# A planner's times set to the trace, and its projections handed out pass by pass

## Chip, cores and metric

One core of a Trainium2 chip runs the whole program. The metric is the time of one execution on the device in microseconds. The kernel before takes 1763.38 us, the median of three runs (1762.12 to 1763.65). The execution that was profiled took 1761.48 us, and its trace, from the first to the last instruction, spans 1759.5 us.

## The reference

Input x is 512 tokens by 1024 channels, fp32. Two transformer layers and a third block run one after the other:

```python
for i in range(2):                                   # first_block
    h, mem_n = _rms_norm(x, ...), _rms_norm(mem, ...)
    if i == 0:  # dilated band attention (12 heads) + attention on 256 memory tokens
        mixed = _attention_sublayer(h, mem_n, att_w_in, att_w_out, rel_bias, mem_w_kv[0])
    else:       # gated delta rule, 6 heads of 128, both directions, chunks of 64, + memory
        mixed = _deltanet_sublayer(h, mem_n, dn_w_in, dn_conv, ..., dn_w_out, mem_w_kv[1])
    x = x + _rms_norm(mixed, ...)
    h = _rms_norm(x, ...)
    x = x + _rms_norm(_swiglu(h, ffn_w_gate_up[i], ffn_w_down[i]), ...)   # width 2816
# second_block: one layer, three mixers beside each other
proj = rmsnorm(x, norm_g) @ w_in
y_gla = gla_mixer(...)      # gated linear attention, chunks of 32
y_s5 = s5_mixer(...)        # diagonal state space, scan over 512 tokens
y_nsa = nsa_mixer(...)      # compressed, selected and windowed attention
x = x + concat(y_gla, y_s5, y_nsa) @ w_out
```

In the delta rule each head solves a unit triangular system per chunk and then carries a state from chunk to chunk, in both directions:

```python
v_new = uc - wc @ state
out = (qc * exp(gc)) @ state + ac @ v_new
state = state * exp(g_last) + (kc * exp(g_last - gc)).T @ v_new
```

## The kernel before, in words

Every large product is done in three fp32r passes: each operand is split into a high and a low part, and `mm3` (L268 to L273) issues low weights by high activations, high by low, and high by high into one PSUM bank. A projection of a piece of 128 output columns over 512 tokens is eight such steps, one for each 128 rows of the weight. The weights come from HBM in pieces of 512 KB, and `weight_stream` (L217) has ScalarE make the high part (L243) and VectorE the low part (L262; GpSimd for a few pieces that are marked `aside`).

No instruction is placed by hand. `Flow` (L56) is a planner that runs while the program is built. Each piece of work is a generator, a thread, which says before each of its steps on which engine it runs and how long it takes (`yield "PE", 0.65`, or `yield act(512)`, `dve(512)`, `pool(512)`, L151 to L160), and issues the step's instructions when the planner hands it on. The planner holds a clock for each engine. A step can start when its engine is free and its inputs are there, which is the end of the producing step plus `HOP`, 0.2 us, where the producer is another engine (`start`, L93; 0.07 us on the same engine, none on TensorE). Of all steps on offer `run` (L99) takes the engine whose step can start first; of that engine's steps that can start within `DELTA`, 0.1 us, of it, the one with the lowest due number (`late`). What comes out is the order of the instructions in each engine's queue. The engines take their queues strictly in that order, and each waits on semaphores for its inputs: the planner's times set the order and nothing else. Rotating buffers and PSUM banks are counted by the same planner (`quota`, `get`, `put`).

The stages: layer 0's attention with its projections (to about 240 us of the trace), its output projection and feed-forward part (to 640), layer 1's delta rule (to 1000), its output projection and feed-forward part (to 1400), the second block (to the end). In the feed-forward stages TensorE has one thread of work. In the delta rule and in the second block, the mixed stages, the `projector` (L1788) is a thread with the due number 20 that offers its projections whenever nothing more urgent can start; the mixers' threads have due numbers from about -9 to 6. Its inner function `part` yields one step for the three passes of an `mm3`, 0.65 us for 512 columns. The output projection and the feed-forward part (`tok_proj`, L967, thread `trunk` with due number 50) yield 0.68 us for an `mm3` and are not touched.

In the delta rule, `inverse` (L1486 on) solves a head's triangular systems in 64 by 64 tiles (L1519 to L1548 by turns of TensorE, ScalarE and VectorE). `chain` carries the state, two threads a head, one for each direction. One chunk of it is

```python
matmul(b[:, 0:P], kT[:, cs], St)                   # PE   L1594
scalar_tensor_tensor(rh, b[:, 0:P], neg, vt, ...)  # DVE  L1597, declared 0.26
matmul(b[:, P:2 * P], Uf[:, d, c, :], rh)          # PE   L1602, declared MM = 0.22
activation(vn, b[:, P:2 * P], AF.Copy)             # ACT  L1605, declared act(128) = 0.21
tensor_scalar(vs, vn, col(ksc, d, c, h), ...)      # DVE  L1610, declared 0.14
matmul(b[:, 2 * P:3 * P], kt[:, c, :], vs)         # PE   L1612
```

and `query` multiplies AT and qe on GpSimd (L1454, L1456, declared `pool(512)` = 1.33). `norm_chain` (L906) ends each sublayer: for each of four groups of 128 tokens a few small VectorE operations (L917, L919, declared 0.1 and 0.07), one on GpSimd (L921, declared 0.47), 512-wide ones on VectorE and ScalarE, again a small one and one on GpSimd (L935, L938), and then TensorE transposes (L949).

Of the kernel before, what the change touches and what calls it, by code (L numbers as in the profile page):

```python
# [49 lines left out]
        self.h, self.l = hi, lo  # L50


DELTA = 0.1


class Flow:  # L56
# [3 lines left out]

    HOP = 0.2

    def __init__(self, **sets):
        self.free = dict.fromkeys(("PE", "ACT", "DVE", "POOL", "DMA"), 0.0)
# [26 lines left out]
    def start(self, eng, toks):  # L93
        s = self.free[eng]
        for at, e in toks:
            s = max(s, at + (self.HOP if e != eng else 0.0 if e == "PE" else 0.07))
        return s

    def run(self):  # L99
        while self.threads:  # L100
            again = True
            while again:
                again = False
                for t in list(self.threads):
                    kind, *arg = t["req"]
                    value = None
                    if kind == "get" and any(self.sets[n] for n in arg):
                        value = min((n for n in arg if self.sets[n]), key=lambda n: min(self.sets[n])[0])
                        tok = min(self.sets[value])
                        self.sets[value].remove(tok)  # L110
                    elif kind == "two" and len(self.sets[arg[0]]) > 1:
                        for _ in range(2):
                            tok = min(self.sets[arg[0]])
                            self.sets[arg[0]].remove(tok)
                    elif kind == "wait" and all(e["tok"] for e in arg):
                        tok = max((e["tok"] for e in arg), key=lambda x: x[0])
                    elif kind == "move" and self.sets[arg[0]]:
                        src, dst = arg
                        tok = min(self.sets[src])
                        self.sets[src].remove(tok)  # L120
                        self.put(dst, tok)
                        tok = t["tok"]
                    elif kind == "late":
                        t["late"] = arg[0]
                        tok = t["tok"]
                    else:
                        continue
                    if tok[0] > t["tok"][0]:
                        t["tok"] = tok
                    self.step(t, value or tok)  # L130
                    again = True
            ops = []
            for t in self.threads:
                if t["req"][0] in self.free:
                    eng, cost, *after = t["req"]
                    ops.append((self.start(eng, after or [t["tok"]]), t))
            assert ops or not self.threads, ([(t["gen"].__name__, t["req"]) for t in self.threads], self.sets, self.free)
            if not ops:
                return
            s, t = min(ops, key=lambda x: x[0])  # L140
            s, t = min((x for x in ops if x[1]["req"][0] == t["req"][0] and x[0] <= s + DELTA), key=lambda x: x[1]["late"])
            eng, cost = t["req"][:2]
            self.free[eng] = s + cost
            t["tok"] = (s + cost, eng)
            self.step(t, t["tok"])
# [17 lines left out]
class K:  # L163
# [132 lines left out]
    def inputs(self, F, W, eX, eM, eF, pro):  # L296
# [93 lines left out]
        def memory():  # L390
            yield "late", 0.5
            for l in range(2):
                yield "wait", *eN[l]
                for c in range(2):
                    ev = W["mk"][l][c]
                    yield "wait", ev
                    yield "get", "mm"
                    p = self.psum("mm")
                    w = ev["W"]
                    for k in range(KT):  # L400
                        t = yield "PE", 0.33
                        self.mm3(p[:, :256], (w.h[:, k, :], w.l[:, k, :]), (M[l].h[:, k, :], M[l].l[:, k, :]),
                                 k == 0, k == KT - 1)
                    F.put("wsl", t)
                    F.add(evac(self.memK[l][:, c, :], p), 0.5, t)
                yield "wait", *W["mv"][l]
                for u in range(2):
                    yield "get", "mm"
                    p = self.psum("mm")
                    ts = slice(u * P, (u + 1) * P)  # L410
                    for k in range(KT):
                        w, kk = W["mv"][l][k // 4]["W"], k % 4
                        t = yield "PE", 0.33
                        self.mm3(p[:, :256], (M[l].h[:, k, ts], M[l].l[:, k, ts]), (w.h[:, kk, :], w.l[:, kk, :]),
                                 k == 0, k == KT - 1)
                    F.add(evac(self.memV[l][:, u, :], p, l == 1 and u == 1), 0.5, t)
                for _ in range(2):
                    F.put("wsl", t)
# [120 lines left out]
    def attention(self, F, W, eX, eM, eB, at, e2):  # L539
# [41 lines left out]
        def group(g):  # L581
# [37 lines left out]
            for i, t0 in enumerate((0, 64, 192, 320, 384)):  # L619
                yield "get", "mm"  # L620
                p = self.psum("mm")
                for k in range(KT):
                    w, kk = W2[k // 4]["W"], k % 4
                    t = yield "PE", 0.33
                    self.mm3(p[:, :256], (X.h[:, k, t0:t0 + P], X.l[:, k, t0:t0 + P]), (w.h[:, kk, :], w.l[:, kk, :]),
                             k == 0, k == KT - 1)
                F.add(copy_v(g, i, p[:, :256], r["t"][2][:, i, :], "mm"), g - 0.5, t)
# [394 lines left out]
    def out_ffn(self, F, i, W, gnext, groups, kev, before):  # L1022
# [57 lines left out]
        for part, (f0, f1) in enumerate(self.PARTS):  # L1080
# [22 lines left out]
            while f < nf:  # L1103
                fs = (f, f + 1) if part == 0 and f == 0 else (f,)
                banks = {}
                for hv in ((0, 256), (256, 512)) if len(fs) == 2 else ((0, 512),):
                    t0, t1 = hv
                    for u in range(t0 // P, t1 // P):
                        yield "wait", eX[u]
                    for f_ in fs:  # L1110
                        for z in range(2):
                            ev = gu[part][f_][z]
                            yield "wait", ev
                            if (f_, z) not in banks:
                                nm = yield "get", *self.ANY
                                banks[f_, z] = self.psum("bk"), nm
                            p = banks[f_, z][0]
                            for k in range(KT):
                                tk = yield "PE", 0.65 * (t1 - t0) / 512
                                self.mm3(p[:, t0:t1], (ev["W"].h[:, k, :], ev["W"].l[:, k, :]),  # L1120
                                         (X.h[:, k, t0:t1], X.l[:, k, t0:t1]), k == 0, k == KT - 1)
                            if t1 == S:
                                F.put("wsl", tk)
                        if t1 == S:
                            F.add(evac_gu(f_, (banks[f_, 0], banks[f_, 1], tk)))
                f += len(fs)
                if part == 0 and f == 4:
                    yield "DMA", 1.4
                    r["post"], _ = row("rowA", a["norm_ffn_post"][i])
                    yield "DMA", 1.4  # L1130
                    r["gain"], _ = row("rowB", gnext)
                    r["ev"] = [F.event() for _ in range(4)]
                    r["eX"] = [F.event() for _ in range(4)]
                    r["store"] = True
                    n4[:] = [0] * 4
# [634 lines left out]
    def proj(self, F, ev, eX, m=P):  # L1770
# [7 lines left out]
        for t0, t1 in rngs:  # L1778
            yield "wait", *eX[t0 // P:t1 // P]
            for k in range(KT):  # L1780
                t = yield "PE", 0.65 * (t1 - t0) / S
                self.mm3(p[:m, t0:t1], (W.h[:, k, :], W.l[:, k, :]), (X.h[:, k, t0:t1], X.l[:, k, t0:t1]),
                         k == 0, k == KT - 1)
        F.put("wsl", t)
# [3 lines left out]
    def projector(self, F, items, eX, eP, late=20, haste=0):  # L1788
# [3 lines left out]

        X = self.X
        yield "late", late

        def part(it, t0, t1):
            W, m = it["W"], it["args"][4]
            yield "wait", *eX[t0 // P:t1 // P]  # L1800
            for k in range(KT):
                t = yield "PE", 0.65 * (t1 - t0) / S
                self.mm3(it["p"][:m, t0:t1], (W.h[:, k, :], W.l[:, k, :]), (X.h[:, k, t0:t1], X.l[:, k, t0:t1]),
                         k == 0, k == KT - 1)
            if t1 == S:
                F.put("wsl", t)
                it["done"]["tok"] = t
# [11 lines left out]
        for i, it in enumerate(items):  # L1819
# [13 lines left out]
            for u in range(4):  # L1833
# [3 lines left out]
                sl = slice(u * P, (u + 1) * P)  # L1837
                for k in range(KT):
                    W, kk = it[k // 4]["W"], k % 4
                    t = yield "PE", 0.33  # L1840
                    self.mm3(p[:, :256], (X.h[:, k, sl], X.l[:, k, sl]), (W.h[:, kk, :], W.l[:, kk, :]),
                             k == 0, k == KT - 1)
                evac, late_ = it[0]["use"]["f"]
# [392 lines left out]
    def s5(self, F, W, eX, open_, eY, uT):  # L2236
# [140 lines left out]
        def glu():  # L2377
# [14 lines left out]
            for c in range(2):  # L2392
                zs = []
                for o in (2, 0):
# [1 line left out]
                    p = self.psum("lv", "glu")  # L2396
                    os_ = slice((o + c) * P, (o + c + 1) * P)
                    for k in range(2):
                        t = yield "PE", 0.65
                        self.mm3(p, (w.h[:, k, os_], w.l[:, k, os_]), yh[k], k == 0, k == 1)  # L2400
                    zs.append((p, t))
                if c:
# [896 lines left out]
```

## Time and profile before

| | |
|---|---|
| median of three runs | 1763.38 us |
| the profiled execution | 1761.48 us |
| its span, first to last instruction | 1759.5 us |
| mean granted TensorE clock | 0.993 of 2.4 GHz |
| TensorE, matmuls | 1708.7 us busy (97%) |
| VectorE | 979.8 us (56%) |
| ScalarE | 763.2 us (43%) |
| GpSimd | 338.0 us (19%) |

Matmuls are pipelined and their ends are modelled: the record of one reaches past the start of the next, and the distance from start to start says what a pass takes of the engine. A short wait of TensorE hides in that overlap, and only a longer one shows as idle time. PE is TensorE's matmuls, PEld its weight loads, DVE VectorE, ACT ScalarE, POOL GpSimd. In names such as bk<-Xh,wl the output stands first, then what is streamed and what is loaded.

### The profile page before, as it was taken

The page shows a single profiled execution, that of the slowest core. Times are in us where ns is not written, and L with a number is a line of the kernel's source. Part 1 is how long each engine was busy: PE and PEld are TensorE (multiplying, and loading weights), DVE is VectorE, ACT ScalarE, POOL GpSimd, SP SyncE. Part 2 cuts the span into 40 slices and gives each one's busy share as a digit, 9 for nine tenths or more (in the row PEclk, how much of TensorE's full clock was granted, in tenths as well). Part 3 has the DMA queues.
Part 4 walks back from the last instruction along what each step waited for, and adds up shares of the span by engine and source line. Part 5 has one row for each costly group of instructions (what it writes and reads, how often), then busy time and mean ns, then how long its engine had stood idle before and what let it go on. Part 6 is the DMA issues. An engine that isn't in the chain of part 4 may idle for free.

```text
span 1759.5 us, 30190 instructions
## 1 busy us (share of the span) xinstructions
PE 1708.7 (97%) x12031; PEld 1423.2 (81%) x12031; DVE 979.8 (56%) x1997; ACT 763.2 (43%) x1808; POOL 338.0 (19%) x496
## 2 busy tenths in 40 slices
PE   6999999999999999999999899999999999999999
PEld 5988679888888888788777788888888888888787
DVE  6333656323333378867887467464433468467573
ACT  5443635333223245656555355333223353345671
POOL 5200001000000021220222351364540033210000
PEclk9999999999999999999999999999999999999999
DMA  6513133333233332211110164345333253552012
GB/s 195 154 51 95 49 120 97 120 96 96 96 96 96 96 114 79 61 38 38 38 37 32 59 152 139 109 133 144 108 108 96 77 159 115 153 154 69 25 37 84
DMA packets 211981, 167.84 MB, mean 95 GB/s; under 512 B 21996, under 2 KB 183036, under 8 KB 211840
## 3 DMA queue, kind: packets, MB, share of 16 engines
q1 hardware_dynamic: 203808, 154.39, 29.7%
q0 software_dynamic: 4560, 9.42, 2.1%
q10 hardware_dynamic: 3472, 2.10, 0.4%
q8 instruction: 94, 1.54, 0.4%
q14 instruction: 47, 0.39, 0.1%
HBM read 152.23 MB, written 13.65 MB: 94 GB/s over the span
## 4 chain that ended last, share of the span: by engine, by line
PE 84%; DVE 9%; ACT 2%; issue 2%; DMA 1%; POOL 1%; ACTq 0%; SPq 0%; DVEq 0%; POOLq 0%
PE bk L271 23%; PE bk L272 22%; PE bk L273 22%; DVE hn L1324 2%; DVE wl L262 1%; PE no L2753 1%; PE npT L2736 1%; PE x L1519 1%; PE x L1523 1%; PE y L1544 1%; DVE hs L942 1%; PE ns L2722 1%; PE hT L949 1%; PE ns L2720 1%; PE o L1625 1%
## 5 line engine op out<-in xcount | busy, mean ns | idle before, releaser
L262 DVE TENSOR_TENSOR wl<-raw,wh 128x512 fp32r<-128x512 f32 x450 | 315.8, 742 | 372.4 <-ACT wh L243 371.8
L243 ACT ACTIVATE wh<-raw 128x512 fp32r<-128x512 f32 x474 | 273.0, 623 | 534.4 <-PE bk L273 300.4
L271 PE MATMUL bk<-Xh,wl 128*128 128x512 f32 (+2 forms) x1312 | 494.9, 377 | 0.2 <-ACT Xh L951 0.2
L272 PE MATMUL bk<-Xl,wh 128*128 128x512 f32 (+2 forms) x1312 | 478.4, 365 | 0.5 <-DVE Xl L956 0.5
L273 PE MATMUL bk<-Xh,wh 128*128 128x512 f32 (+2 forms) x1312 | 478.5, 365 | 0.0
L273 PEld LDWEIGHTS bk<-Xh,wh 128*128 128x128 f32 (+1 forms) x1312 | 246.9, 188 | 40.1
L271 PEld LDWEIGHTS bk<-Xh,wl 128*128 128x128 f32 (+1 forms) x1312 | 247.5, 189 | 39.0 <-issue 3.5
L272 PEld LDWEIGHTS bk<-Xl,wh 128*128 128x128 f32 (+1 forms) x1312 | 247.7, 189 | 34.8 <-DVE Xl L956 0.9
L271 PE MATMUL bk<-wh,Xl 128*128 128x512 f32 (+1 forms) x424 | 152.6, 360 | 6.7 <-DVE Xl L796 3.7
L272 PE MATMUL bk<-wl,Xh 128*128 128x512 f32 (+1 forms) x424 | 145.8, 344 | 0.3 <-DVE wl L262 0.2
L273 PE MATMUL bk<-wh,Xh 128*128 128x512 f32 (+1 forms) x424 | 145.2, 342 | 0.0
L271 PE MATMUL bk<-wh,Al 128*128 128x512 f32 x352 | 139.7, 397 | 0.0
L272 PE MATMUL bk<-wl,Ah 128*128 128x512 f32 x352 | 139.5, 396 | 0.0
L921 POOL TENSOR_TENSOR nc<-ncm,nhalf 128x1 f32<-128x1 f32 x16 | 11.5, 720 | 661.9 <-DVE ncm L919 661.9
L273 PE MATMUL bk<-wh,Ah 128*128 128x512 f32 x352 | 138.6, 394 | 0.0
L1093 DVE TENSOR_TENSOR sg<-sg,bk 128x512 f32<-128x512 f32 x44 | 30.2, 687 | 124.7 <-PE bk L273 120.2
L271 PEld LDWEIGHTS bk<-wh,Xl 128*128 128x128 f32 x424 | 84.7, 200 | 18.0 <-DVE Xl L796 3.1
L273 PEld LDWEIGHTS bk<-wh,Xh 128*128 128x128 f32 x424 | 84.8, 200 | 8.1
L272 PEld LDWEIGHTS bk<-wl,Xh 128*128 128x128 f32 x424 | 85.0, 200 | 7.6 <-DVE wl L262 1.0
L271 PEld LDWEIGHTS bk<-wh,Al 128*128 128x128 f32 x352 | 66.0, 188 | 16.1
L273 PEld LDWEIGHTS bk<-wh,Ah 128*128 128x128 f32 x352 | 66.0, 188 | 16.0
L272 PEld LDWEIGHTS bk<-wl,Ah 128*128 128x128 f32 x352 | 66.1, 188 | 15.4
(586 smaller groups left out, 2623.8 us busy)
## 6 DMA issues: line engine op xcount, KB each, us to landing
raw<-in_ffn_w_gate_up_dram SPq DMA_DIRECT2D x88, 512.0 KB, 3.9
raw<-in_ffn_w_down_dram SPq DMA_DIRECT2D x44, 512.0 KB, 3.3
raw<-in_dn_w_in_dram SPq DMA_DIRECT2D x27, 512.0 KB, 4.0
raw<-in_att_w_in_dram SPq DMA_DIRECT2D x20, 512.0 KB, 4.1
raw<-in_w_in_dram SPq DMA_DIRECT2D x20, 512.0 KB, 3.8
raw<-in_mem_w_kv_dram SPq DMA_DIRECT2D x8, 512.0 KB, 3.6
raw<-in_att_w_out_dram SPq DMA_DIRECT2D x8, 512.0 KB, 3.3
xd<-x SPq DMA_DIRECT2D x8, 512.0 KB, 2.6
```

Of the source, the lines that this page charges most:

```text
L243: nc.scalar.activation(wh[:, sl], ev["raw"][:, sl], AF.Copy)
L262: eng.tensor_tensor(wl[:, sl], raw[:, sl], wh[:, sl].bitcast(F32), op=OP.subtract)
L271: mm(out, A[1], B[0], start=first, stop=False, **kw)
L272: mm(out, A[0], B[1], start=False, stop=False, **kw)
L273: mm(out, A[0], B[0], start=False, stop=last, **kw)
L942: nc.vector.scalar_tensor_tensor(hh[:, hv[i]], x[:, t, hv[i]], r2, r["gain"][:, hv[i]], op0=OP.mult, op1=OP.mult)
L949: nc.tensor.transpose(p[:, k * P:(k + 1) * P], hh[:, i * 512 + k * P:i * 512 + (k + 1) * P], self.ident)
L1093: nc.vector.tensor_tensor(sg, sg, pu, op=OP.mult)
L1324: nc.vector.scalar_tensor_tensor(acc[:, d0:d1], raw[:, d0 + o:d1 + o], cw[:, ti, tap:tap + 1], acc[:, d0:d1], op0=OP.mult, op1=OP.add)
L1519: nc.tensor.matmul(dn8(b[i])[at], lhsT, rhs, start=True, stop=True)
L1523: nc.tensor.transpose(b[d][:, o:o + P], U[:, d, 2 * n:2 * n + 2, :].rearrange("p c q -> p (c q)"), self.ident)
L1544: nc.tensor.matmul(dn8(ys[par])[HB[f], d, n, :], T[d][HB[par], n, f, :], xs[f][HB[par], d, n, :], start=True, stop=True)
```

## The change

The planner's numbers are replaced: `DELTA` 0.05 for 0.1; between engines 0.2 us from TensorE, 0.12 us to TensorE and 0.04 us otherwise, and nothing on the same engine; each step on VectorE costs 0.08 us and each on ScalarE 0.07 us more than it says; an `mm3` of 512 columns is 0.682 us (was 0.65), of 256 columns in the token-major projections 0.36 us (was 0.33). GpSimd's and the DMAs' declared times and the numbers that steps of the mixers declare for TensorE stay. In `projector`, `part` yields for each pass by itself, so that the planner can put other TensorE steps between the passes of one product; the passes, their order among themselves and their banks are the same.

```diff
-DELTA = 0.1
+DELTA = 0.05
...
-    HOP = 0.2
+    HOP = 0.04
+    FROM_PE, TO_PE = 0.2, 0.12
+    STEP = {"DVE": 0.08, "ACT": 0.07}
...
     def start(self, eng, toks):
         s = self.free[eng]
         for at, e in toks:
-            s = max(s, at + (self.HOP if e != eng else 0.0 if e == "PE" else 0.07))
+            s = max(s, at + (self.FROM_PE if e == "PE" else self.TO_PE if eng == "PE" else self.HOP) * (e != eng))
...
             eng, cost = t["req"][:2]
+            cost += self.STEP.get(eng, 0.0)
             self.free[eng] = s + cost
...
# front, token-major projections, projector's token-major pieces
-                        t = yield "PE", 0.33
+                        t = yield "PE", 0.36
...
# gate/up projections, proj, glu
-                t = yield "PE", 0.65 * (t1 - t0) / S
+                t = yield "PE", 0.682 * (t1 - t0) / S
...
# projector
         def part(it, t0, t1):
             W, m = it["W"], it["args"][4]
             yield "wait", *eX[t0 // P:t1 // P]
             for k in range(KT):
-                t = yield "PE", 0.65 * (t1 - t0) / S
-                self.mm3(it["p"][:m, t0:t1], (W.h[:, k, :], W.l[:, k, :]), (X.h[:, k, t0:t1], X.l[:, k, t0:t1]),
-                         k == 0, k == KT - 1)
+                for i, (w, x) in enumerate(((W.l, X.h), (W.h, X.l), (W.h, X.h))):
+                    t = yield "PE", 0.2275 * (t1 - t0) / S
+                    nc.tensor.matmul(it["p"][:m, t0:t1], w[:, k, :], x[:, k, t0:t1], start=k == i == 0,
+                                     stop=k == KT - 1 and i == 2)
```

## Rows read from the trace of the kernel before

**Rows 1.** The page's head, and its busy times by engine.

```profile
span 1759.5 us, 30190 instructions
PE 1708.7 (97%) x12031; PEld 1423.2 (81%) x12031; DVE 979.8 (56%) x1997; ACT 763.2 (43%) x1808; POOL 338.0 (19%) x496
```

**Rows 2.** By stage: stretch, length, then busy us by engine, clock, DMA, GB/s.

```profile
200.00:240.00 40.00, 33.02 (x281) 24.64 (x280) 30.00 (x75) 21.52 (x72) 0.00 (x0) 0.96 0.09 28
240.00:640.00 400.00, 399.56 (x1858) 331.70 (x1857) 158.43 (x262) 132.55 (x257) 7.79 (x12) 1.00 0.34 104
640.00:690.00 50.00, 44.23 (x296) 39.56 (x295) 41.63 (x82) 26.38 (x63) 12.63 (x12) 0.97 0.43 121
690.00:1000.00 310.00, 299.50 (x3656) 245.98 (x3654) 235.39 (x538) 174.67 (x477) 68.92 (x56) 0.99 0.14 40
1440.00:1715.00 275.00, 273.06 (x2476) 227.28 (x2475) 182.01 (x405) 148.78 (x392) 38.64 (x43) 1.00 0.35 98
```

**Rows 3.** Groups by line, 690 to 1000: count, busy us and mean ns, idle before.

```profile
L271 PE MATMUL bk<-Xh,wl 128*128 128x512 f32 x170 | 76.2, 448 | 0.0
L1612 PE MATMUL chain<-vs,ktok 128*128 128x128 f32 x72 | 14.5, 297 | 5.4 <-DVE vs L1610 5.3
```

**Rows 4.** TensorE in order of time: start, duration, line, instruction.

```profile
800.67 0.40 PE L273 MATMUL bk<-Xh,wh 128*128 128x512 f32 x1
800.90 0.38 PE L1594 MATMUL chain<-St,kTh 128*128 128x128 f32 x2
...
801.84 0.50 PE L271 MATMUL bk<-Xh,wl 128*128 128x512 f32 x1
802.18 0.39 PE L272 MATMUL bk<-Xl,wh 128*128 128x512 f32 x1
```

**Rows 5.** Waits of TensorE, 690 to 1000: us in total, times, longest.

```profile
PE chain L1612 <- DVE vs L1610: 5.3, 5, 1.4
```

**Rows 6.** Line L1610 in the whole trace: shortest, median and longest duration.

```profile
L1610 DVE TENSOR_SCALAR vs<-vn,ksc x36: 269/280/1299, 744.6 to 993.6; 128x128 f32<-128x128 f32 x36
```

**Rows 7.** A stall in order of time: TensorE, then VectorE, then GpSimd.

```profile
942.13 0.49 PE L1612 MATMUL chain<-vs,ktok 128*128 128x128 f32 x2 [1.33 <-DVE vs L1610]
...
940.79 2.50 DVE L1610 TENSOR_SCALAR vs<-vn,ksc 128x128 f32<-128x128 f32 x2
...
940.28 1.71 POOL L1456 TENSOR_TENSOR qe<-qe,qTh 128x512 f32<-128x512 f32 x1
941.95 1.26 POOL L1454 TENSOR_TENSOR AT<-AT,kq 128x512 f32<-128x512 f32 x1
```

**Rows 8.** A stretch of low clock, columns of rows 2, and TensorE in it.

```profile
864.50:867.80 3.30, 3.30 (x28) 2.79 (x30) 2.43 (x7) 0.79 (x2) 0.00 (x0) 0.50 0.00 0
943.10:946.40 3.30, 3.05 (x13) 2.84 (x14) 3.27 (x7) 0.28 (x1) 1.33 (x2) 0.50 0.00 0
...
865.08 0.63 PE L272 MATMUL bk<-Xl,wh 128*128 128x512 f32 x1
865.50 0.63 PE L273 MATMUL bk<-Xh,wh 128*128 128x512 f32 x1
```

**Rows 9.** One turn of the state's chain, in order of time.

```profile
987.47 0.39 PE L1594 MATMUL chain<-St,kTh 128*128 128x128 f32 x2
...
987.73 0.28 ACT L1605 ACTIVATE vn<-chain 128x128 f32<-128x128 f32 x1 [0.70 <-PE chain L1602]
...
988.16 0.28 DVE L1610 TENSOR_SCALAR vs<-vn,ksc 128x128 f32<-128x128 f32 x1
```

**Rows 10.** A norm chain in order of time, and its GpSimd step's group.

```profile
644.20 0.15 DVE L919 TENSOR_SCALAR ncm<-ncm 128x1 f32<-128x1 f32 x1
644.50 0.54 POOL L921 TENSOR_TENSOR nc<-ncm,nhalf 128x1 f32<-128x1 f32 x1 [0.94 <-DVE ncm L919]
645.08 1.77 DVE L925 SCALAR_TENSOR_TENSOR x<-y,nc,x 128x512 f32<-128x512 f32 x1
...
L921 POOL TENSOR_TENSOR nc<-ncm,nhalf 128x1 f32<-128x1 f32 x16 | 11.5, 720 | 661.9 <-DVE ncm L919 661.9
```

More of the change, by code (lines that the diff above doesn't have):

```diff
@@ L412, in memory @@
                         w, kk = W["mv"][l][k // 4]["W"], k % 4
-                        t = yield "PE", 0.33
+                        t = yield "PE", 0.36
                         self.mm3(p[:, :256], (M[l].h[:, k, ts], M[l].l[:, k, ts]), (w.h[:, kk, :], w.l[:, kk, :]),
@@ L623, in group @@
                     w, kk = W2[k // 4]["W"], k % 4
-                    t = yield "PE", 0.33
+                    t = yield "PE", 0.36
                     self.mm3(p[:, :256], (X.h[:, k, t0:t0 + P], X.l[:, k, t0:t0 + P]), (w.h[:, kk, :], w.l[:, kk, :]),
@@ L1118, in out_ffn @@
                             for k in range(KT):
-                                tk = yield "PE", 0.65 * (t1 - t0) / 512
+                                tk = yield "PE", 0.682 * (t1 - t0) / 512
                                 self.mm3(p[:, t0:t1], (ev["W"].h[:, k, :], ev["W"].l[:, k, :]),
@@ L1788, in projector @@
     def projector(self, F, items, eX, eP, late=20, haste=0):
-        X = self.X
+        X, nc = self.X, self.nc
         yield "late", late
@@ L1839, in projector @@
                     W, kk = it[k // 4]["W"], k % 4
-                    t = yield "PE", 0.33
+                    t = yield "PE", 0.36
                     self.mm3(p[:, :256], (X.h[:, k, sl], X.l[:, k, sl]), (W.h[:, kk, :], W.l[:, kk, :]),
@@ L2398, in glu @@
                     for k in range(2):
-                        t = yield "PE", 0.65
+                        t = yield "PE", 0.682
                         self.mm3(p, (w.h[:, k, os_], w.l[:, k, os_]), yh[k], k == 0, k == 1)
```

## The prediction

> **What bounds the kernel now.** I read the page's head first, then busy time by stage, then inside the mixed stages the waits of TensorE and the order of time around the longest. The head shows TensorE with matmuls in flight for 1708.7 of 1759.5 us [rows 1], so 50.8 us of idle is all that shows. By stage it is uneven: the feed-forward stretch has 0.4 us of it in 400, the delta rule 10.5 in 310 (690 to 1000), the norms at 640 to 690 5.8, the attention's end at 200 to 240 7.0, the second block's mixed part 1.9 in 275 [rows 2]. VectorE, the next engine, is at 235.4 of 310 in the delta rule [rows 2]. So the kernel is bound by TensorE's queue nearly everywhere, and a new order can win only what TensorE loses by standing before an instruction whose input is late while other work lies behind it. The start, the attention's end and the tail run out of such work: no order of projections helps there.
>
> Idle shows only part of the loss. A pass of 512 columns is recorded with 0.40 us, yet the next instruction starts 0.23 later [rows 4]; a wait under about 0.17 us hides in that overlap.
>
> What makes TensorE stand in the delta rule? Half of the 10.5 us is five waits at L1612 for VectorE's L1610, 5.3 us [rows 5]. L1610 takes 0.28 us in the median and 1.30 at worst [rows 6]. In the instance at 942 two of them stretch over 2.50 us while GpSimd runs L1456 and L1454, and TensorE idles 1.33 us before L1612 [rows 7]. After such waits TensorE's clock is at the half level, 1.2 GHz, at 864.5 and 943.1 [rows 8]. In the first, passes follow at 0.42 us instead of 0.23 [rows 4, 8], so 3.3 us of dense work lose 3.3 x (1 - 0.23/0.42) = 1.5.
>
> **The change, part by part.** No instruction is added or taken away: each `mm3` already was three matmuls with three weight loads, and the passes stay in order. Splitting costs nothing by itself where a 128-row small matmul follows a pass: L1594 starts 0.23 us behind L273, as another pass would [rows 4]. Behind the 64 by 64 tiles the first pass takes 0.34 us (801.84 to 802.18 [rows 4]), 0.11 more; each burst of these tiles is one step of the planner's and stays one, so that their number does not grow. I take 0. Bounds: 0, and 0.11 for each of the 170 `mm3` of [rows 3] if a border cost that wherever one is cut, 19 us; the nearer row, an ordinary small matmul, says 0.
>
> The split shortens how long an urgent step stands behind a projection: on average half a step, 0.34 us before and 0.11 after. That is latency of the mixers' chains, which TensorE's filler covers as long as projections last, so I cost it at nothing. Without that cover it would be 0.23 us a visit.
>
> `DELTA`: the planner may leave TensorE idle for up to 0.1 us so that an urgent step goes first, now 0.05. The mean of what can be left is 0.05 and 0.025. L1612's 72 records are 36 turns [rows 3, 9], and a turn has about four TensorE visits, so some 140 visits in the chains. If half of them used the allowance: 70 x 0.025 = 1.7 us won. Bounds 0 and 140 x 0.05 = 7.
>
> The times between engines: a round trip TensorE, VectorE, TensorE is planned with 0.2 + 0.08 + 0.12 = 0.40 us around the operation, 0.2 + 0.2 before: the same. With ScalarE and VectorE between (vn, vs) from the product to the end of vs: 0.2 + 0.28 + 0.04 + 0.22 = 0.74, before 0.2 + 0.21 + 0.2 + 0.14 = 0.75; the trace has 988.16 + 0.28 - 987.47 = 0.97 [rows 9]. So the new table is no nearer there. What it does mend is the load of VectorE and ScalarE, 0.08 and 0.07 us on every step that stood back to back, and projections 5% longer. From this I expect that part of the 5.2 us of delta-rule idle that isn't L1612's goes: I take two fifths, 2.0 us. Bounds: 5.2 won, and as much lost if new mis-orders replace the old.
>
> The collisions of L1610 with GpSimd: the planner keeps each engine's time by itself, before and after, so a new order shifts them by chance. I take 0 for the 5.3 us, bounds 5.3 won and 5.3 lost, with one half-clock stretch more or less for each pair of long waits: 2 x 1.5 either way. The page of the Trainium skill titled SBUF — State Buffer (SBUF: two separate sides) says that VectorE and GpSimd share one pair of ports as an exclusive lock, held for a whole instruction. The stretch of L1610 to 2.50 us for two beside L1456 agrees. By that rule no table of per-engine times can plan these waits away; by the planner's own table they would be gone, and the sum would be 5.3 + 3.0 us lower.
>
> The half-clock stretches: if fewer waits leave one of the two out, 1.5 us; I give it a half, 0.7. The second block has the same edits and 1.9 us of idle: I take 0.5 won, bounds 1.9 won and 3 lost.
>
> The norm chains: VectorE to GpSimd to VectorE was planned as 0.27 + 0.67 = 0.94 us from L919's start to L925's, now 0.19 + 0.51 = 0.70; the trace has 0.88 (644.20 to 645.08) [rows 10]. The transposes behind it may thus be queued 0.18 us too early, twice a chain, 16 chains [rows 10]: 5.8 us lost at most. Against it stands VectorE's longer planned load in the same stretch (41.6 of 50 us busy [rows 2]), which puts them later again. I take 0. If that cover is absent, transposes wait in front of gate/up passes.
>
> The remaining edits, 0.36 and 0.682 in the front and the gate/up stage, act where TensorE has one thread or is dense (399.6 of 400 [rows 2]): 0, bounds 2 either way.
>
> Sum: 1.7 + 2.0 + 0.7 + 0.5 = 4.9 us off the profiled execution, 1761.5 - 4.9 = 1756.6. That execution lies 1.9 below the median of the runs, so 1758.5 for the median.
>
> **Rivals.** *Nothing measurable*: chains that advance faster gain nothing where projections fill in, and the waits that cost are collisions that the table doesn't hold. For it: TensorE's 1.9 us of idle in 275 of the second block [rows 2], and L1612's half of the delta rule's idle [rows 5]. Against it: every queue of the mixed stages is reordered, so exact balance would be chance. 1763, within 3.5.
>
> *A tighter plan stalls more*, the slower side. An urgent step used to stand behind a whole `mm3` in the plan, and that margin, anything from 0 to 0.68 us, absorbed what came late. With passes it is 0 to 0.23. For an input late by 0.2 us (0.97 measured against 0.74 planned [rows 9]) the mean uncovered wait was 0.2 x 0.2/2/0.68 = 0.03 us and becomes 0.09. Over 140 visits 8 us, and with one half-clock stretch more about 9.5: 1772.9. It decides where lateness passes about 0.1 us, half a pass. For it: L1610's waits show that lateness of this size is there. Against it: many waits of 0.1 us hide or vanish in other lateness, and 0.05 less `DELTA` works the other way.
>
> *The collisions fall apart too*: the order moves the chains off GpSimd's L1454 and L1456, and L1612's waits and both half-clock stretches go: 1758.5 less 5.3 and the remaining 2.3 = 1750.9. For it: only five waits make the 5.3 us, so a small shift can miss them. Against it: GpSimd is busy 68.9 of 310 us [rows 2], and VectorE is loaded three quarters, so most shifts meet it again.
>
> *The change doesn't do what it says*: if no urgent step falls between the passes of one `mm3`, only the numbers act; this gives the time of the first rival and is counted with it.
>
> **How the numbers follow.** My forecast 0.34, collisions gone 0.12, nothing 0.25, tighter plan 0.29. About 0.2%, 3.5 us, is what a measurement of this kernel tells from no change. The forecast lies 4.9 below the median, just past that, so some of it falls inside; some of the first rival falls outside on either side. Faster 0.45, same 0.26, slower 0.29. Range: from 1745, below the collision rival by the bound of `DELTA` (7 instead of 1.7), to 1775, just above the tighter plan; beyond lie the far bounds (all norm chains late, 0.11 us at every border), less than 2 in 10 with both ends. The forecast's own range is 1753 to 1762.
>
> **What would show it.** In the changed trace, small TensorE steps between an L271-type pass and the next of the same product; TensorE's idle at 690 to 1000 near 8 us instead of 10.5; L1612's waits on L1610 still there, at other places; one half-clock stretch in the delta rule instead of two; feed-forward stretches unchanged in length. Many short waits of 0.1 to 0.3 us before chain matmuls would show the tighter plan. The prediction is wrong if the delta rule's length changes by more than 8 us, or if the time moves in a stage that has no projector.

## The result: 1780.15 us, 1.0% slower

The changed kernel takes 1780.15 us, the median of 4 runs (1779.62 to 1780.54), against 1762.75 of the kernel before beside it: a ratio of 1.0104, 95% interval 1.0085 to 1.0123. Forecast were 1758.5 and a range to 1775, so both the sign and the range were wrong.

The head of the page of the changed kernel, answering to [rows 1]:

```profile
span 1777.3 us, 30180 instructions
PE 1713.0 (96%) x12031; PEld 1426.1 (80%) x12031; DVE 974.9 (55%) x1997; ACT 759.1 (43%) x1804; POOL 335.7 (19%) x496
```

The span grew by 17.8 us. TensorE's matmuls are in flight 4.3 us longer, so most of the loss is idle TensorE. By stage, with the columns of [rows 2], and a stretch from the start that [rows 2] doesn't have:

```profile
0.00:50.00 50.00, 30.53 (x138) 24.09 (x139) 26.09 (x43) 25.17 (x45) 20.78 (x32) 0.86 0.59 173
200.00:240.00 40.00, 34.50 (x271) 26.57 (x271) 25.04 (x63) 21.57 (x78) 0.00 (x0) 0.87 0.08 28
240.00:640.00 400.00, 393.56 (x1865) 326.45 (x1862) 158.27 (x261) 130.89 (x249) 5.54 (x8) 1.00 0.33 102
1440.00:1715.00 275.00, 272.12 (x2472) 229.69 (x2471) 180.71 (x390) 143.96 (x356) 44.30 (x50) 1.00 0.38 107
```

The first of these stretches in the kernel before:

```profile
0.00:50.00 50.00, 35.46 (x210) 30.52 (x211) 31.26 (x45) 29.21 (x55) 29.03 (x36) 0.93 0.67 196
```

The delta rule, on which the prediction spent its words, takes as long as it did: 311.2 us in both kernels from its first instruction to the last product into a chain's state (L1612, now L1615), called the last chain step below. The first 50 us lost 4.9 us of busy TensorE. The stretches are 10 to 18 us later in the program than the same numbers were before, so what ends at 240 isn't the same work; the comparison that stands is when the same instruction starts. The first projection of x starts 10.2 us later than before (59.8 against 49.6), the last scores of layer 0's attention (`as`) 13.6 later, layer 0's last down product 13.5, the delta rule's last chain step 14.3, layer 1's first down product 18.1, the end 17.8. So most was lost in the first 60 us, some at the attention's end, some between the delta rule and layer 1's down projection.

**The start.** The planner's numbers also order the queues that feed TensorE. SyncE's holds the loads of x and of the weights; in the kernel before, two loads of x stand between those of the memory's last five weights (columns: start, duration, queue, line, load):

```profile
17.25 0.38 SPq L207 DMA_DIRECT2D raw<-in_mem_w_kv_dram  x1
17.68 0.51 SPq L318 DMA_DIRECT2D xs<-in_x_dram  x1
21.81 7.72 SPq L207 DMA_DIRECT2D raw<-in_mem_w_kv_dram  x3
29.58 0.50 SPq L318 DMA_DIRECT2D xs<-in_x_dram  x1
33.13 0.37 SPq L207 DMA_DIRECT2D raw<-in_mem_w_kv_dram  x1
```

In the changed kernel all four loads of x come ahead of these five, which then drag from 20.71 to 45.94: a load needs one of three buffers (`raw`), and a buffer comes free only when the high and low parts of the weight in it are made.

```profile
7.54 4.40 SPq L321 DMA_DIRECT2D xs<-in_x_dram  x4
20.71 25.23 SPq L210 DMA_DIRECT2D raw<-in_mem_w_kv_dram  x5
```

The steps of x's norms now stand ahead of the weights in more than one queue. ScalarE makes no high part between 28.10 and 41.48 us: its queue has x's evacuations (L387) first and stands before one of them for 4.00 us. GpSimd's low parts begin at 37.19 us (22.16 before), though high parts for them lay ready from 28.10 on: GpSimd's queue has the small steps of x's norms (L343) first and stands before the last of them for 4.90 us, then before a step for the attention's bias for 2.07. ScalarE, then GpSimd of the changed kernel:

```profile
26.96 1.14 ACT L246 ACTIVATE wh<-raw 128x512 fp32r<-128x512 f32 x2
36.50 0.60 ACT L387 ACTIVATE Xh<-hT 128x512 fp32r<-128x512 f32 x1 [4.00 <-PE hT L357]
...
33.37 0.54 POOL L343 TENSOR_TENSOR irs<-iss,nhalf 128x1 f32<-128x1 f32 x1 [4.90 <-DVE iss L341]
37.19 3.77 POOL L265 TENSOR_TENSOR wl<-raw,wh 128x512 fp32r<-128x512 f32 x3
```

GpSimd of the kernel before:

```profile
22.16 5.24 POOL L262 TENSOR_TENSOR wl<-raw,wh 128x512 fp32r<-128x512 f32 x3
```

The DMA queues starve meanwhile. From 20 to 40 us (columns of [rows 2]; the last is GB/s) in the changed kernel, and in the kernel before:

```profile
20.00:30.00 10.00, 7.43 (x33) 5.37 (x34) 8.95 (x16) 8.08 (x16) 2.40 (x3) 0.96 0.15 52
30.00:40.00 10.00, 7.86 (x34) 6.21 (x35) 6.60 (x11) 2.50 (x5) 4.49 (x7) 0.53 0.20 55
```

```profile
20.00:30.00 10.00, 7.62 (x49) 5.93 (x47) 9.48 (x12) 7.71 (x17) 8.77 (x7) 1.00 0.51 165
30.00:40.00 10.00, 9.63 (x51) 8.21 (x52) 4.95 (x10) 3.77 (x8) 7.69 (x8) 0.66 0.57 187
```

The Trainium skill calls the queues of ScalarE, VectorE and GpSimd strict FIFO (PSUM — Partial Sum Buffer, "Engine vs sequencer instructions"). ScalarE's 4.00 us and GpSimd's 4.90 us of standing, with weights waiting behind, agree.

**The norm chains.** In layer 1's first one, TensorE's queue has the transposes of the last token group much too early. Between the third group's transposes and the fourth's stand 21 passes of 256 columns, where the kernel before has 54. At the 0.12 us that such a pass takes from start to start, the 33 passes are 4.0 us. VectorE's `hs` (L945), which the transposes need, did come sooner, 5.66 us after the third group's instead of 7.99, but only by 2.3 us; TensorE waits 1.73 us for it. VectorE, then TensorE of the changed kernel, and the same of the kernel before:

```profile
1059.86 1.41 DVE L945 SCALAR_TENSOR_TENSOR hs<-x,nc,rowB 128x512 f32<-128x512 f32 x2
1065.52 1.41 DVE L945 SCALAR_TENSOR_TENSOR hs<-x,nc,rowB 128x512 f32<-128x512 f32 x2 [0.46 <-POOL nc L941]
...
1060.75 0.63 PE L952 MATMUL hT<-ident,hs 128*128 128x128 f32 x4
1066.42 0.63 PE L952 MATMUL hT<-ident,hs 128*128 128x128 f32 x4 [1.73 <-DVE hs L945]
```

```profile
1043.24 1.41 DVE L942 SCALAR_TENSOR_TENSOR hs<-x,nc,rowB 128x512 f32<-128x512 f32 x2
1051.23 1.41 DVE L942 SCALAR_TENSOR_TENSOR hs<-x,nc,rowB 128x512 f32<-128x512 f32 x2 [0.69 <-POOL nc L938]
...
1044.22 0.60 PE L949 MATMUL hT<-ident,hs 128*128 128x128 f32 x4
1052.29 0.60 PE L949 MATMUL hT<-ident,hs 128*128 128x128 f32 x4
```

In layer 0's first norm chain the fourth group's transposes stand behind 39 passes instead of 51; there TensorE waits 0.84 us for a weight's low part and 0.51 us for `hs`.

**The delta rule.** The same work in both kernels, from its first instruction to the last chain step, and from there to the last head's `poT`, the transposes of its output (columns of [rows 2]; the changed kernel first):

```profile
697.50:1008.70 311.20, 304.56 (x3672) 248.87 (x3673) 234.50 (x542) 177.27 (x485) 69.12 (x57) 0.99 0.14 40
1008.70:1016.20 7.50, 2.94 (x22) 2.42 (x20) 2.18 (x9) 1.83 (x10) 2.09 (x3) 0.96 0.17 70
```

```profile
683.20:994.40 311.20, 300.70 (x3646) 246.52 (x3647) 239.54 (x541) 176.54 (x484) 70.49 (x57) 0.98 0.14 40
994.40:1003.40 9.00, 8.08 (x48) 6.72 (x47) 2.35 (x9) 1.84 (x10) 2.10 (x3) 1.00 0.16 59
```

TensorE idles 6.6 us in the first of these stretches, 10.5 before. Its 26 more matmuls there say where the gain went: 24 of them are passes of the layer's output projection, done sooner, and in the second stretch TensorE has 22 matmuls left where it had 48, and stands. Behind it, TensorE waits 2.0 us for a weight's high part (L246), which the kernel before doesn't. The waits of TensorE from 700 on, answering to [rows 5] with their columns (L1615 and L1613 are the former L1612 and L1610, L1522 the former L1519), and its one stretch at the lower clock inside the delta rule, with the columns of [rows 2]:

```profile
PE chain L1615 <- DVE vs L1613: 3.1, 5, 1.7
PE x L1522 <- DVE U L1551: 2.6, 2, 1.7
PE poT L1338 <- POOL otok L1661: 4.4, 1, 4.4
```

```profile
981.50:984.90 3.40, 3.40 (x37) 2.90 (x31) 1.21 (x3) 1.93 (x4) 0.00 (x0) 0.50 0.38 144
```

The planner does put other steps between the passes (L1807) of a product, in time:

```profile
803.57 0.39 PE L1597 MATMUL chain<-St,kTh 128*128 128x128 f32 x2
803.80 0.39 PE L1628 MATMUL o<-vn,AT 128*128 128x128 f32 x2
803.94 0.48 PE L1807 MATMUL bk<-Xh,wh 128*128 128x512 f32 x1
804.26 0.38 PE L1597 MATMUL chain<-St,kTh 128*128 128x128 f32 x2
804.39 0.48 PE L1807 MATMUL bk<-Xh,wl 128*128 128x512 f32 x1
804.71 0.38 PE L1605 MATMUL chain<-rhs,Uf 128*128 128x128 f32 x2
```

A pair of small matmuls and the pass behind it take 0.45 us here (804.26 to 804.71). A pair among small ones takes 0.23 (803.57 to 803.80), a pass among passes 0.23 [rows 4]. So putting a step between two passes cost nothing: the pass behind it counts 0.32 us from start to start, and the pair before it only 0.13.

### The profile page after: what moved, and what is told of

It is laid out like the page before. It is cut to its first block, busy times and chain, and to the rows that moved or that the text cites. A ratio compares the mean times of both kernels' runs of the same rounds, so it can differ in the third digit from the quotient of the medians.

```text
span 1777.3 us, 30180 instructions
## 1 busy us (share of the span) xinstructions
PE 1713.0 (96%) x12031; PEld 1426.1 (80%) x12031; DVE 974.9 (55%) x1997; ACT 759.1 (43%) x1804; POOL 335.7 (19%) x496
## 4 chain that ended last, share of the span: by engine, by line
PE 86%; DVE 8%; ACT 2%; issue 1%; DMA 1%; POOL 1%; SPq 0%; DVEq 0%; ACTq 0%; POOLq 0%
PE bk L274 19%; PE bk L275 18%; PE bk L276 18%; PE bk L1807 11%; DVE wl L265 2%; PE x L1522 1%; PE x L1526 1%; PE no L2757 1%; PE npT L2740 1%; PE y L1547 1%; DVE hs L945 1%; PE ns L2726 1%; PE ns L2724 1%; PE o L1628 1%; PE chain L1605 1%
## 5 line engine op out<-in xcount | busy, mean ns | idle before, releaser
L265 DVE TENSOR_TENSOR wl<-raw,wh 128x512 fp32r<-128x512 f32 x450 | 322.2, 755 | 387.4 <-ACT wh L246 386.5
L246 ACT ACTIVATE wh<-raw 128x512 fp32r<-128x512 f32 x474 | 273.0, 622 | 546.8 <-PE bk L276 279.4
L274 PE MATMUL bk<-Xh,wl 128*128 128x512 f32 (+1 forms) x912 | 338.3, 371 | 0.8 <-DVE wl L265 0.8
L276 PE MATMUL bk<-Xh,wh 128*128 128x512 f32 (+1 forms) x912 | 334.7, 367 | 0.0
L275 PE MATMUL bk<-Xl,wh 128*128 128x512 f32 (+1 forms) x912 | 334.6, 367 | 0.0
L274 PEld LDWEIGHTS bk<-Xh,wl 128*128 128x128 f32 x912 | 171.9, 189 | 30.4 <-issue 1.8
L276 PEld LDWEIGHTS bk<-Xh,wh 128*128 128x128 f32 x912 | 171.9, 188 | 28.5
L275 PEld LDWEIGHTS bk<-Xl,wh 128*128 128x128 f32 x912 | 172.0, 189 | 27.2 <-issue 0.2
L1807 PE MATMUL bk<-Xh,wh 128*128 128x512 f32 (+2 forms) x400 | 149.7, 374 | 0.0
L1807 PE MATMUL bk<-Xh,wl 128*128 128x512 f32 (+2 forms) x400 | 148.7, 372 | 0.0
L1807 PE MATMUL bk<-Xl,wh 128*128 128x512 f32 (+2 forms) x400 | 148.1, 370 | 0.0
```

The costliest lines, as they stand in the source:

```text
L246: nc.scalar.activation(wh[:, sl], ev["raw"][:, sl], AF.Copy)
L265: eng.tensor_tensor(wl[:, sl], raw[:, sl], wh[:, sl].bitcast(F32), op=OP.subtract)
L274: mm(out, A[1], B[0], start=first, stop=False, **kw)
L275: mm(out, A[0], B[1], start=False, stop=False, **kw)
L276: mm(out, A[0], B[0], start=False, stop=last, **kw)
L1807: nc.tensor.matmul(it["p"][:m, t0:t1], w[:, k, :], x[:, k, t0:t1], start=k == i == 0, stop=k == KT - 1 and i == 2)
```

## The experiments

All runs use the changed kernel with a switch by stage: 1 plans a stage with the new numbers and passes, 0 with the old ones. The stages are, in this order, start (x's and the memory's norms and projections), attention, layer 0's output projection and feed-forward part, delta rule, layer 1's output projection and feed-forward part, second block.

```diff
+    STAGES, SPLIT, stage = (0, 1, 1, 1, 1, 1), (0, 1, 1, 1, 1, 1), 0
...
         for at, e in toks:
+            if not self.STAGES[self.stage]:
+                s = max(s, at + (0.2 if e != eng else 0.0 if e == "PE" else 0.07))
+                continue
...
-... x[0] <= s + DELTA) ...
+... x[0] <= s + (0.1, DELTA)[self.STAGES[self.stage]]) ...
...
-            cost += self.STEP.get(eng, 0.0)
+            cost += self.STEP.get(eng, 0.0) * self.STAGES[self.stage]
```

The TensorE steps are switched likewise, and `SPLIT` chooses passes or whole products. The cuts below show their two values alone. Differences below are the ratio less one, times 1763 us.

**Only the start old** (`STAGES` and `SPLIT` as shown).

> The changed kernel, but the planner keeps the old numbers (table, DELTA, durations) until the memory tokens' projections are handed out, and takes the new ones from there on. Theory S (the loss is made in the first 60 us, where the new numbers put all four loads and norms of x ahead of the memory weights: the first projection of x starts 10.2 us later in the changed trace): 1770, within 3. Theory T (the tighter plan makes TensorE stand in the mixed stages): 1778 to 1781, as the changed kernel.

Measured: 1771.75 us, ratio 1.0052 (1.0037 to 1.0067), +9.2. The first projection of x is back at 49.7. So the start makes 18.3 - 9.2 = 9.1 us of the loss, and about as much lies behind it.

**Only the start new.**

```diff
-(0, 1, 1, 1, 1, 1), (0, 1, 1, 1, 1, 1)
+(1, 0, 0, 0, 0, 0), (1, 0, 0, 0, 0, 0)
```

> The kernel before, with the new numbers only until the memory tokens' projections are handed out; everything after by the old numbers and without the split into passes. Theory S: 1773, within 3, the first projection of x near 59.8 us instead of 49.6. Theory T: 1763, within 2.

Measured: 1771.44 us, 1.0041 (1.0027 to 1.0055), +7.2. The first projection of x starts at 60.7, 11.1 late; later stages keep that distance within about 2 us. No stage with a projector is changed here.

**The numbers without the split, and the split without the numbers.**

```diff
-(1, 1, 1, 1, 1, 1), (1, 1, 1, 1, 1, 1)
+(1, 1, 1, 1, 1, 1), (0, 0, 0, 0, 0, 0)    # the numbers alone
+(0, 0, 0, 0, 0, 0), (1, 1, 1, 1, 1, 1)    # the passes alone
```

> All new numbers, but the projector hands out a whole mm3 in a step, as before. Theory S: 1778 to 1781, since the startup has no projector. Theory T: 1763 to 1768, since it is the split that takes the margin away.

> All old numbers, and only the projector's split into passes (0.2275 us each). Theory S: 1763, within 3. Theory T: 1770 or more.

Measured: 1784.95 us (1.0125, 1.011 to 1.014) for the numbers alone, 1773.13 us (1.0057, 1.0042 to 1.0072) for the passes alone. The two don't add: 22 and 10 us against 18 together. In the second block, from layer 1's last transposes to the end, the numbers alone lose 8.2 us, the passes alone 7.6, and both together 0.2. Why the second block bears one of them so badly wasn't followed up. The numbers alone lie above both times that were expected of them; the passes alone came out as the tighter plan had it, 1770 or more. In their profile 6.5 us of the loss lie between the delta rule's last chain step and layer 1's first down product, and the 7.6 us in the second block. The passes alone show what the split does for the chains: in the delta rule the output transposes of heads 0, 1 and 2 come 11, 21 and 35 us earlier than before, and yet the last chain step comes only 1.6 us earlier.

**The start new, three norms of x later.** The cause supposed above was tried by itself. The norms of x's last three groups get due numbers of 0.9 to 1.1, so that they no longer pass the memory's weights. This moves their steps on every engine.

```diff
-                F.add(norm(i), -2 + 0.1 * i, xs[i][1])
+                F.add(norm(i), -2 + 0.1 * i if i < 3 else 0.6 + 0.1 * i, xs[i][1])
```

> As e2_startup_new (new numbers in the startup alone), but the norms of x's second to fourth token groups have due numbers of 0.9 to 1.1 instead of -1.7 to -1.5, so that ScalarE's queue makes the memory weights' high parts before it evacuates x. Theory S (the ten us are the memory weights standing behind x in ScalarE's queue, with the three raw buffers full and the DMAs idle): 1762 to 1766, the first projection of x back near 50 us. Rival S' (the new numbers cost the startup in another way, in VectorE's or TensorE's order): 1770 to 1773, as e2.

Measured: 1761.16 us, 0.9991 (0.9982 to 1.0001). The loss of the run with only the start new is gone. The five loads of memory weights are done by 35.92, the low parts start at 21.66, and the DMA moves 127 and 168 GB/s at 20 to 40 us instead of 52 and 55. SyncE, GpSimd, and the stretch from 20 us of this run:

```profile
20.65 15.27 SPq L214 DMA_DIRECT2D raw<-in_mem_w_kv_dram  x5
...
21.66 3.48 POOL L269 TENSOR_TENSOR wl<-raw,wh 128x512 fp32r<-128x512 f32 x2
```

```profile
20.00:30.00 10.00, 8.83 (x45) 6.94 (x45) 9.21 (x14) 6.12 (x12) 6.30 (x5) 1.00 0.45 127
30.00:40.00 10.00, 10.00 (x81) 9.26 (x80) 0.55 (x1) 4.38 (x9) 8.74 (x10) 1.00 0.52 168
```

SyncE still loads x first here; so the place of x's norms in the engines' queues, not the order of the loads, is what cost. The run moves the norms in all queues at once and doesn't tell ScalarE's from GpSimd's or VectorE's. Nor did a run tell which of the new numbers (`DELTA`, the times between engines, the longer steps, 0.36) had moved them.

**The attention, the delta rule, the second block, each alone.**

```diff
+(0, 1, 0, 0, 0, 0), (0, 1, 0, 0, 0, 0)    # attention
+(0, 0, 0, 1, 0, 0), (0, 0, 0, 1, 0, 0)    # delta rule
+(0, 0, 0, 0, 0, 1), (0, 0, 0, 0, 0, 1)    # second block
```

> New numbers only from the end of the startup to the end of layer 0's attention. Theory S with a second place (the attention loses too: 5.1 us between the first projection of x and the end of layer 0 in e1_startup_old, 3.3 in the changed kernel): 1767 to 1769. If what e1 showed there was only a consequence of later changes or chance: 1762 to 1764.

> New numbers and the split only from the end of layer 0's feed-forward part to the end of the delta rule. The prediction's step (less idle of TensorE in the delta rule): 1759 or less. Theory P (TensorE is the bound and projections fill in, so faster chains move work inside the stage and what idles is moved to its end): 1763 to 1767, the stage from the last transpose of layer 0's norm to the first down-projection of layer 1 449 to 453 us against 449.4. Theory T (tighter plan): 1770.

> New numbers and the split only in the second block. From the changed kernel (that stage 0.2 us longer than before): 1763. From e3 and e4 (numbers or split alone, that stage 8 us longer): the split and the numbers alone mis-order it, both together do not; so 1762 to 1765 by that, and 1770 if the loss there belongs to either of them in any company.

Measured: the attention 1765.45 us (1.0012, 1.0003 to 1.0022), +2.1; the delta rule 1761.53 (0.9990, 0.9980 to 0.9999), -1.8; the second block 1762.72 (0.9997, 0.9988 to 1.0006), -0.5. In the first, TensorE stands before a head's scores for `kT`, then before `ms_t` and `mo`, and the granted clock (the column with 0.50, a share of 2.4 GHz) is then at its lower level, 1.2 GHz, for 6.8 us:

```profile
204.62 0.94 PE L666 MATMUL as<-kT,qT 64*128 64x128 f32 x12 [2.21 <-ACT kT L585]
206.38 1.94 PE L890 MATMUL ms_t<-ident,mp 128*128 128x128 f32 x8 [0.82 <-DVE mp L881]
208.73 1.98 PE L906 MATMUL mo<-mpT,memV 128*64 128x128 f32 x16 [0.41 <-DVE mpT L896]
```

```profile
206.20:209.60 3.40, 2.81 (x16) 2.44 (x18) 3.33 (x10) 1.43 (x6) 0.00 (x0) 0.50 0.17 65
209.60:213.00 3.40, 3.40 (x22) 2.57 (x20) 1.15 (x2) 2.62 (x13) 0.00 (x0) 0.50 0.02 5
```

The same three waits (2.21, 0.72, 0.41 us) stand in the whole change, and the kernel before has 1.30 before its scores there. In the delta rule alone, heads finish up to 11 us earlier, the last chain step 2.0 and the stage 0.5 us earlier: TensorE spends its projections sooner and then stands 4.4 us before the last head's `poT` for GpSimd's `otok`, 0.9 in the kernel before. Stage lengths of single profiles carry about 2 us of scatter: the run with only the second block new, whose delta rule is planned as before, spans 313.2 us there against 311.2.

**Both feed-forward stages alone.**

```diff
+(0, 0, 1, 0, 1, 0), (0, 0, 1, 0, 1, 0)
```

> The new numbers (and nothing else of the change, since these stages have no projector) only while the planner is in the two output projections, norm chains and feed-forward parts; the start, the attention, the delta rule and the second block are planned with the old ones. Theory A (the 8 us of the changed kernel that the start, the attention, the delta rule and the second block taken singly don't account for come from these stages, as the prediction's bound for the norm chains has it: transposes queued 0.18 us too early, up to 5.8): 1768 to 1771, the loss at 640 to 700 and 1010 to 1060. Theory B (dense stages have one order whatever the numbers are; the loss needs the new delta rule before it): 1762 to 1764.5.

Measured: 1768.26 us, 1.0034 (1.0023 to 1.0046), +6.0. These stages have no projector. The waits (time, line, idle before, releaser) are those of the whole change, all absent before:

```profile
287.24 0.39 PE L278 MATMUL bk<-Xh,wl 128*128 128x256 f32 x1 [0.84 <-DVE wl L269]
289.79 0.63 PE L957 MATMUL hT<-ident,hs 128*128 128x128 f32 x4 [0.51 <-DVE hs L950]
...
1056.01 0.63 PE L957 MATMUL hT<-ident,hs 128*128 128x128 f32 x4 [1.73 <-DVE hs L950]
```

Between the same instructions (first transposes of the norm chain to the first down product), the 64 third passes of 256 columns take 7.7 us from start to start in the kernel before, in both layers, and 9.7 and 9.9 here (a late transpose behind a pass lengthens this distance): 4.2 us, in the first norm chain of each layer. The expectation had layer 0's loss at 640 to 700; nothing was lost there. The other 1.8 us aren't placed: in this profile 2.5 us go at the delta rule's last head, whose plan is the old one.

**Everything behind the attention new.**

```diff
+(0, 0, 1, 1, 1, 1), (0, 0, 1, 1, 1, 1)
```

> The change in everything behind the attention (both feed-forward parts, delta rule, second block); the start and the attention old. The run with only the start old took 1771.75 and the one with only the attention new 1765.45. Theory A (effects of stages add): 1763 + (1771.75 - 1765.45) = 1769, with about 4 us lost between the delta rule's last chain step and the first product of layer 1's down projection (TensorE waiting 4.4 us for otok at the delta rule's end, 0.9 before). Theory B (that loss needs the attention's new order, through the order in which later weights and buffers come): 1761 to 1764.

Measured: 1768.40 us, 1.0039 (1.0027 to 1.0052), +6.9: the loss needs nothing of the attention or the start. The profiled execution, 1765.02 us, was the shortest of five; in it 1.9 us, not 4, are lost between the last chain step and layer 1's first down product, 3.0 between the attention's last scores and layer 0's first down product, and the 4.4 us before `poT` are there.

**The whole change, three norms of x later.**

```diff
+(1, 1, 1, 1, 1, 1), (1, 1, 1, 1, 1, 1)
-                F.add(norm(i), -2 + 0.1 * i, xs[i][1])
+                F.add(norm(i), -2 + 0.1 * i if i < 3 else 0.6 + 0.1 * i, xs[i][1])
```

> The whole change, with one edit besides: the norms of the last three groups of x have due numbers 0.9 to 1.1 in place of -1.7 to -1.5, which undid the loss at the start where the new numbers were there alone. Theory A (the loss at the start adds to the rest): 1780.2 less 8.7 to 10 = 1770 to 1772, first projection of x near 51 in place of 59.8. Theory B (what the start loses is slack that a later stage would have lost anyway, or the later order depends on it): 1775 to 1781 though the first projection of x comes near 51.

Measured: 1770.80 us, 1.0057 (1.0042 to 1.0071), +10.0. Three due numbers win back 18.3 - 10.0 = 8.3 us.

**The stages that don't lose.**

```diff
+(1, 0, 0, 1, 0, 1), (1, 0, 0, 1, 0, 1)    # and the three norms later
```

> The new numbers and passes in the start (with the norms of x's last three groups later), in the delta rule and in the second block; the old ones in the attention and both feed-forward parts. If the single effects add (start mended -1.6, delta rule -1.7, second block -0.5): 1759 to 1760, faster than both kernels. If a stage's order, once shifted, meets the next stage's in another place (as the second block lost 7 to 8 us with passes alone and with numbers alone, and nothing with both): anywhere from 1759 to 1770, most of the difference in a stage whose own numbers are unchanged from the run with that stage alone.

Measured: 1758.47 us, the median of 12 runs, against 1762.58; ratio 0.9977 (0.9968 to 0.9986), 4.1 us faster than the kernel before and some 22 faster than the whole change. It is the forecast's time, but by chance: it comes from a part of the change, with the start mended.

## Why the prediction was wrong

| part of the change, alone | us, from the ratio | interval | the prediction's term |
|---|---|---|---|
| start | +7.2 | 4.8 to 9.7 | 0, "bounds 2 either way" |
| attention | +2.1 | 0.5 to 3.9 | the same term |
| both feed-forward stages | +6.0 | 4.1 to 8.1 | 0, up to 5.8 lost |
| delta rule | -1.8 | -3.5 to -0.2 | -4.4 |
| second block | -0.5 | -2.1 to 1.1 | -0.5 |
| sum | +13.0 | | -4.9 |
| the whole change | +18.3 | 15.0 to 21.7 | |

The parts leave 5.3 us of the whole; the six intervals' half-widths, as the root of their squares, are 5.4, so this may be measurement, or an interplay that the runs don't resolve.

**The step that failed** is "act where TensorE has one thread or is dense ... 0, bounds 2 either way", with "no order of projections helps there" ahead of it. That term measured +7.2 us at the start alone and +2.1 at the attention. It asked where a new order could help TensorE, not where it could hurt, and it counted only 0.36 and 0.682 as acting there, though the new `DELTA`, times between engines and step costs act on the start as well. The planner's numbers order the queues of ScalarE, VectorE, GpSimd and SyncE too, and where TensorE runs out of work, at the start, their order is the critical path. No line of `norm(i)`, which hands out x's norms, is changed, and yet the planner moved them past the memory's weights. The profile before could have shown the risk: at 20 to 40 us its DMA moves 165 and 187 GB/s, its TensorE is idle for 2.75 us, and three `raw` buffers stand between the two.

**The norm chains** were seen with mechanism and bound ("transposes behind it may thus be queued 0.18 us too early ... 5.8 us lost at most") and then set to 0 for "VectorE's longer planned load". The mechanism was there and the cover wasn't: the new plan moved the last group's transposes forward in TensorE's queue, by 33 passes or 4.0 us in layer 1, while VectorE's `hs` came 2.3 us sooner. The loss, 6.0 us, came as a few waits up to 1.73 us, not as 32 of 0.18. Which of the new numbers made the plan so early there stays open.

**The delta rule** was right in kind. Splitting costs nothing by itself (0.45 us for a pass and a pair of small matmuls, 0.23 and 0.23 apart); the 0.34 us that the prediction read for a pass behind 64 by 64 tiles is a distance from start to start too, and how much of it is a price wasn't measured. L1610's waits fell from 5.3 to 3.1 us, those before L1522 for U rose from 1.8 to 2.8: collisions moved by chance, as the term of 0 said. L1613's longest is 1.307 us, near the 1.299 of [rows 6], and lies beside GpSimd's L1459; so the exclusive lock that the prediction cited from the Trainium skill (SBUF — State Buffer) still fits. TensorE's idle up to the last chain step fell from 10.5 to 6.6 us, more than to the forecast's 8, and two stretches at the lower clock became one. What failed is that less idle meant less time. The 3.9 us went into passes of the output projection, done sooner; heads are up to 11 us earlier in the run with the delta rule alone (35 with the passes alone), and at the last head the filler that the chains overtook is missing: 4.4 us before `poT`, 0.9 before. The prediction said "TensorE's filler covers as long as projections last" and didn't ask what stands at the end. Of the 4.4 us forecast for the stage, the run with the delta rule alone won 1.8.

**The rival "a tighter plan stalls more"** had a time near the result's side, 1772.9, but its place was wrong: many short waits in the chains didn't appear, and the delta rule and the second block alone aren't slower. Under the old numbers it isn't refuted: the passes alone took 1773.13 us, with the loss at the delta rule's end and in the second block, not in the chains. The prediction's own test, "or if the time moves in a stage that has no projector", came true in the start and in both feed-forward stages.

**The clock** may have added to it. The granted clock is 0.988 over 1777.3 us and was 0.993 over 1759.5: (1 - 0.988) x 2 x 1777.3 = 43 us at the lower level against 25. Where TensorE was busy all through, 18 more such us are worth at most half of that, 9 us, already within the losses above. This isn't shown to be its price: the four runs of the changed kernel had granted clocks from 0.983 to 0.991, 28 us apart by the same sum, and lie within 0.9 us of each other. The prediction had counted such stretches only for the delta rule.

## What to carry to other kernels

Numbers of a planner are global: before costing them, list every queue that the planner orders, and look first at the stretches where the bounding engine idles, since there another engine's queue is the critical path. A term that has a mechanism and a bound on one side, and only a hope on the other, is to be entered with part of its bound, not with 0. After a change has shifted a program, a window of the same times holds other work: compare from instruction to instruction; here that showed 3.9 us less idle, which the window of 690 to 1000 hid, with 300.15 us of busy TensorE against 299.50. Try such a change stage by stage: here parts of it win 4.1 us and the whole loses 18.3.

## What the runs showed of the chip

Short waits of TensorE were followed by a lower clock: behind 2.21 and 0.82 us of idle at the attention's end TensorE ran 6.8 us at 1.2 GHz, twice as long as the 3.3 us of [rows 8]. The rate of the DMA queues in the start went with the free buffers: 52 and 55 GB/s while the weights stood in the three buffers, and 321 in the 10 us before, when the loads had buffers.
